# A hybrid encoder layer on one core: the scan's output step in its PSUM banks, six groups with both pairs of chunks in one run, and a split last product

## The chip, the core and the metric

The kernel runs on one core of a Trainium2 chip. The metric is device time in microseconds (us), lower is better: one layer of an encoder on 512 tokens of width 1024, batch 1, in float32. An execution is timed from outside; the profile shows one execution of its own, whose span runs from its first to its last recorded instruction.

TensorE multiplies matrices into PSUM, in banks of 128 x 512 float32, of which there are eight. VectorE (DVE) and ScalarE (ACT) read and write SBUF and PSUM; in this kernel GpSimd (POOL) works on SBUF alone. SyncE (SP) issues nearly all transfers. Each engine takes its instructions in order and waits at semaphores for the others.

## The reference

The layer mixes tokens by two branches, a bidirectional chunked state-space scan ("SSD") and windowed attention, merges them by gates, projects, normalises, adds the residual, and then runs a squared-ReLU MLP. The change touches the end of the scan and the end of the MLP:

```python
def ssd_scan(x, dt, a, b, c):           # one direction, 4 chunks of 128 tokens, 8 groups g of 4 heads
    ...
    cb = jnp.einsum('bclgn,bcsgn->bcgls', c, b)
    y_diag = jnp.einsum('bcgls,bcgrls,bcsgrp->bclgrp', cb, decay, xdt)      # within a chunk
    ...
    y_off = jnp.einsum('bclgn,bcgrpn,bcgrl->bclgrp', c, prev, jnp.exp(a_cs))
    return (y_diag + y_off).reshape(Bsz, S, G, R, P)

def ssd_branch(z, xbc, dt_raw, ...):
    ...
    y = y_fwd + y_bwd + xs * d_skip
    y = gated_rmsnorm(y, z, norm_w)     # u = y * silu(z); u * rsqrt(mean(u*u) per group) * w
    return y @ w_out

f = jnp.square(jax.nn.relu(h @ w_mlp_in)) @ w_mlp_out
x = x + rmsnorm(f, post_mlp_norm)
```

`prev` holds the states that enter each chunk from the ones before it. All matrix products are computed from float32 operands: each operand is split into a high part and a low part, and three products hi·hi, hi·lo, lo·hi are added in PSUM (`mm3`). The names `wh`/`wl`, `fh`/`fl`, `th`/`tl` are such pairs; `fc` holds both parts of one.

## The kernel before, in words

**What runs.** A list of "quanta" is built, each with weight chunks and a piece of TensorE work. The input projection comes first; then, for g = 0 to 7, six projections of the scan group g + 1 stand beside the scan steps of group g, attention heads, gates and the attention's output; then the scan's output projection, the output projection "o", the MLP's up projection, and its down projection in four parts, each a Winograd-Strassen product of seven half-size products. Part 3 is the program's end.

**Scan group g.** `prep(c)` makes for each of four chunks the decay matrix `m`. `load(c)` brings `E`, the factors exp(a_cs) of one or two directions (two for the two middle entries, so six 128x256 blocks per group). `off(j)` multiplies, for the pair j of two chunks, the entering states `pv` by `C` into two PSUM banks `yo`; `scaled(j)` (line 1207) has VectorE write `yo * E` over `E` in SBUF, which frees the bank. `diag(j)` multiplies `m` and `x` into one bank `yd` with 64-column tiles. `joined(j)` (line 1213) has VectorE add `yd` to `w` (which holds x times d_skip), then POOL add each block of `E` (line 1219) and multiply by the gate `z` (line 1220). ScalarE squares, POOL adds the squares (1227), and `rms` and `finish` normalise. `outs(0)` and `outs(1)` (line 1235) place these steps for the two pairs; in the groups of the table `JOINED` the first visit does only `off(0)` and `scaled(0)`, and the second all the rest of both pairs. `outs` also runs the attention's value products that are due (`ps<-pT,V` in a trace).

**Banks.** Three banks are called `pp` (projections), five `ps` (everything else). A name in a trace is the name of the tensor.

**The end.** In part 3 the seven products run in the order A11, A12, S2, S1, S4, S3, A22, each for two blocks of 128 tokens (u = 0, 1), 12 matmuls of 512 columns a block. They accumulate in banks X, Y and Z. After each block `gather` (line 1666) adds the bank to an SBUF tile `acc`. When the last product of an output block is in, `down_done` (line 1675) squares `acc` with a row sum on ScalarE (1686), adds the sums (1689, 1691), multiplies by the norm's gains into `ag` (1695), and, when both halves of a token row are there, has POOL raise the mean to -1/2 (1698) and VectorE compute `x1 + ag * r` (1701), which SP writes out (1702).

**Order.** After the program is written, `Planner` puts each engine's instructions in a fixed order by dependencies, estimated durations and due times; what an engine runs next is then fixed, and it waits if the operand is late. Uses of one PSUM bank count as dependent on each other whatever their columns.

## Time and profile before

| | us |
|---|---|
| median of 3 runs (1071.22 to 1071.63) | 1071.27 |
| the profiled execution, timed from outside | 1071.39 |
| its span | 1069.4 |
| HBM read | 128.68 MB |

A row of the profile reads "line engine operation out<-in, shapes, xcount", then busy time and the mean of one. A row of the timeline reads: start, duration, engine, line, operation, and in brackets the idle time before it with the engine that ended it. "PEld" is TensorE's loading of the stationary operand, beside its matmuls. Matmuls are pipelined: the duration that stands in a row (about 0.39 us for 512 columns) overlaps the next one, so the distance of two starts tells what one costs. Some matmul records are missing from a trace.

### The profile page before, as it was taken

To read this page: it belongs to the slowest core of one execution; us is meant where nothing else is said; L and a number is where in the kernel's file an instruction comes from. 1 tells how busy PE (TensorE), PEld (TensorE's weight loads), DVE (VectorE), ACT (ScalarE), POOL (GpSimd) and SP (SyncE) were. 2 spreads that over 40 slices of the span, in tenths; PEclk is the share of its full clock that TensorE was granted. 3 is DMA by queue.
4 is the path that set the end of the run, shared out by engine and by line. 5 is a ranking of instruction groups with operands and counts; after the bars stand their busy time and mean duration, and the time that the engine had idled before them with its cause. 6 is when DMAs were issued, how large, how long until landed. Compare 5 with 4: busy or idle time off the path is not lost.

```text
span 1069.4 us, 16514 instructions
## 1 busy us (share of the span) xinstructions
PE 1059.7 (99%) x5542; PEld 894.1 (84%) x5542; DVE 774.7 (72%) x1352; ACT 658.4 (62%) x1411; POOL 770.3 (72%) x862
## 2 busy tenths in 40 slices
PE   9999999999999999999999999999999999999997
PEld 8888888888888888888888888889888888888885
DVE  5987877886895878788876536798764584584698
ACT  7875776686686767677787414566645444444552
POOL 4746457477577698998789956214688897898994
PEclk9999999999999999999999999999999999999999
DMA  8433323433433526253535444317222421424122
GB/s 323 136 128 110 98 99 115 132 99 118 127 110 124 158 94 173 75 178 126 176 88 176 156 142 138 128 65 242 90 69 80 157 79 65 155 97 150 67 99 78
DMA packets 62084, 134.24 MB, mean 126 GB/s; under 512 B 9128, under 2 KB 18984, under 8 KB 62000
## 3 DMA queue, kind: packets, MB, share of 16 engines
q1 hardware_dynamic: 61712, 132.96, 38.3%
q8 instruction: 43, 0.70, 0.3%
q14 instruction: 41, 0.34, 0.1%
q10 hardware_dynamic: 288, 0.23, 0.1%
HBM read 128.68 MB, written 4.49 MB: 125 GB/s over the span
## 4 chain that ended last, share of the span: by engine, by line
PE 90%; DVE 5%; DMA 2%; ACT 2%; issue 1%; POOL 0%; DVEq 0%; POOLq 0%; ACTq 0%
PE pp L455 57%; PE ps L455 30%; PE ps L459 3%; DMA row<-in_row 1%; DMA x<-in_x 1%; DVE P L952 1%; DVE u L1014 1%; DMA xt<-in_xt 0%; DVE h L746 0%; POOL wl L1621 0%; DMA wr<-in_wv 0%; ACT P L946 0%; DVE dtw L817 0%; DVE Q L911 0%; DVE x L1416 0%
## 5 line engine op out<-in xcount | busy, mean ns | idle before, releaser
L534 POOL TENSOR_TENSOR wl<-wr,wh 128x342 fp32r<-128x342 f32 (+2 forms) x390 | 385.7, 1004 | 209.5 <-ACT wh L530 200.8
L455 PE MATMUL pp<-h,wh 128*128 128x512 f32 (+1 forms) x1664 | 505.5, 385 | 0.0
L455 PEld LDWEIGHTS pp<-h,wh 128*128 128x128 f32 x1664 | 306.4, 188 | 59.4 <-issue 0.7
L455 PE MATMUL pp<-h,wl 128*128 128x512 f32 (+1 forms) x832 | 320.8, 386 | 0.0
L530 ACT CAST wh<-wr 128x1024 fp32r<-128x1024 f32 (+1 forms) x130 | 135.0, 1040 | 127.6 <-PE pp L455 102.6
L455 PEld LDWEIGHTS pp<-h,wl 128*128 128x128 f32 x832 | 156.4, 188 | 30.5 <-issue 0.2
L1621 POOL TENSOR_TENSOR wl<-wd,wh 128x256 fp32r<-128x256 f32 x158 | 133.4, 882 | 12.5 <-ACT wh L1618 12.1
L1618 ACT CAST wh<-wd 128x512 fp32r<-128x512 f32 x92 | 53.3, 618 | 36.2 <-PE ps L455 19.3
L455 PE MATMUL ps<-wl,fh 128*128 128x512 f32 x184 | 71.7, 390 | 0.1
L455 PE MATMUL ps<-wh,fh 128*128 128x512 f32 x184 | 71.6, 389 | 0.0
L455 PE MATMUL ps<-wh,fl 128*128 128x512 f32 x184 | 71.6, 389 | 0.0
L1456 DVE SCALAR_TENSOR_TENSOR pp<-pp,r 128x256 f32<-128x256 f32 (+1 forms) x31 | 17.3, 559 | 64.6 <-ACT r L1453 64.5
L1180 ACT ACTIVATE n<-cb,tables 128x128 f32<-128x128 f32 x128 | 49.1, 392 | 17.6 <-DVE cb L1171 17.6
L1014 DVE SCALAR_TENSOR_TENSOR u<-pp,cv,u 128x510 f32<-128x510 f32 (+1 forms) x64 | 47.8, 746 | 7.1 <-ACT u L1010 5.7
L1181 ACT ACTIVATE m<-cb,tables 128x128 f32<-128x128 f32 x128 | 48.8, 389 | 2.3 <-DVE cb L1171 2.3
L1219 POOL TENSOR_TENSOR w<-w,E 128x256 f32<-128x256 f32 x48 | 41.7, 880 | 7.5 <-DVE w L1215 6.5
L1174 POOL TENSOR_TENSOR rb<-rb,tables 128x512 f32<-128x512 f32 x32 | 37.8, 1185 | 7.3 <-DMA rb<-csT 6.0
L1176 ACT ACTIVATE rf<-rf,tables 128x128 f32<-128x128 f32 x128 | 41.9, 392 | 1.8 <-DMA rf<-csT 1.7
L1112 POOL TENSOR_TENSOR xd<-x,tables 128x256 f32<-128x256 f32 x48 | 34.8, 742 | 9.1 <-ACT x L1037 3.5
L455 PEld LDWEIGHTS ps<-wl,fh 128*128 128x128 f32 x184 | 34.5, 188 | 8.0 <-POOL wl L1621 0.6
L455 PEld LDWEIGHTS ps<-wh,fh 128*128 128x128 f32 x184 | 34.5, 188 | 7.2
L455 PEld LDWEIGHTS ps<-wh,fl 128*128 128x128 f32 x184 | 34.5, 188 | 7.0
(291 smaller groups left out, 2262.4 us busy)
## 6 DMA issues: line engine op xcount, KB each, us to landing
wr<-in_w_in_b SPq DMA_DIRECT2D x74, 512.0 KB, 4.7
wr<-in_w_mlp_in_b SPq DMA_DIRECT2D x32, 512.0 KB, 3.3
wd<-in_w_mlp_out SPq DMA_DIRECT2D x64, 256.0 KB, 3.6
rb<-csT SPq DMA_DIRECT2D x32, 256.0 KB, 4.1
rf<-csT SPq DMA_DIRECT2D x32, 256.0 KB, 4.3
wr<-in_w_ssd_out_b SPq DMA_DIRECT2D x13, 512.0 KB
x<-in_x SPq DMA_DIRECT2D x16, 256.0 KB, 4.3
E<-csE SPq DMA_DIRECT2D x32, 128.0 KB, 4.4
```

The costliest lines, as they stand in the source:

```text
L455: self.nc.tensor.matmul(out, lhsT, rhs, start=start, stop=stop, skip_group_check=more)
L530: self.nc.scalar.copy(hi[:, :m], raw)
L534: self.nc.gpsimd.tensor_tensor(lo[:, c], raw[:, c], hi[:, c].bitcast(F32), op=ALU.subtract)
L1014: nc.vector.scalar_tensor_tensor(u[:, a:e], ps[:, a + d:e + d], self.wtap(t, b), u[:, a:e], op0=ALU.mult, op1=ALU.add)
L1112: nc.gpsimd.tensor_tensor(v4(xd[:, d * 256:(d + 1) * 256]), v4(xs(c)), by_dir(self.coef, c)[:, d].unsqueeze(2).to_broadcast([128, 4, 64]), ...
L1174: nc.gpsimd.tensor_tensor(v4(rb), v4(rb), cs[:, 1].unsqueeze(2).to_broadcast([128, 4, 128]), op=ALU.subtract)
L1176: nc.scalar.activation(v4(rf)[:, h], v4(rf)[:, h], AF.Identity, bias=ncs[:, 0, h:h + 1])
L1180: nc.scalar.activation(v4(n)[:, h], cb[:, 0], AF.Copy, scale=dt[:, 0, h:h + 1])
L1181: nc.scalar.activation(v4(m)[:, h], cb[:, 1], AF.Copy, scale=dt[:, 1, h:h + 1])
L1219: nc.gpsimd.tensor_tensor(wc, wc, E[:, d], op=ALU.add)
L1618: nc.scalar.copy(hi, src)
L1621: (nc.vector if q == 512 else nc.gpsimd).tensor_tensor(lo[:, c], src[:, c], hi[:, c].bitcast(F32), op=ALU.subtract)
```

## The change

Three things. (1) For all eight groups, `scaled` multiplies inside the bank `yo`, gives `E` back at once, and VectorE adds each block of `yo` to `w`; `joined` adds `w` into the bank `yd` and VectorE writes `yd * z` to `w`. POOL's two lines are left without callers. `scaled(j)` now stands right behind `off(j)`. (2) Groups 0 and 5 join 3, 4, 6, 7 in `JOINED`. (3) The last three products of part 3 become one quantum with their six blocks in the order of `CLOSING`. The last block is done in two halves of 256 columns, the far half in a bank of its own. Where a bank is not used again, `acc` is added into the bank, not the bank to `acc` (`summed`), and the norm's gains are multiplied in place there; otherwise they go to a `pp` bank. The unchanged context that the diff leaves out is marked by "...".

```diff
...
 PAIRS = (1, 0), (2, 3)
-JOINED = (3, 4, 6, 7)
+JOINED = (0, 3, 4, 5, 6, 7)
 ALONE = (7,)
...
 BACK = 3
+IN_BANK = range(8)
+END, END_BANK = 256, "ps"
+CLOSING = ("S4", 0), ("S3", 0), ("S4", 1), ("A22", 0), ("S3", 1), ("A22", 1)
 PIECES = 3
...
                 dd = slice(dirs[3 - c][0], dirs[3 - c][-1] + 1)
-                E = ch[c]["E"]
-                nc.vector.tensor_tensor(E[:, dd], ch[c]["yo"][:, dd], E[:, dd], op=ALU.mult)
+                E, yo = ch[c]["E"], ch[c]["yo"]
+                if g not in IN_BANK:
+                    nc.vector.tensor_tensor(E[:, dd], yo[:, dd], E[:, dd], op=ALU.mult)
+                    continue
+                nc.vector.tensor_tensor(yo[:, dd], yo[:, dd], E[:, dd], op=ALU.mult)
+                put(E)
+                for d in dirs[3 - c]:
+                    wc = st["w"][j][:, c % 2]
+                    nc.vector.tensor_tensor(wc, yo[:, d], wc, op=ALU.add)
 
         def joined(j):
             w = st["w"][j]
-            nc.vector.tensor_tensor(w, ch[j]["yd"], w, op=ALU.add)
-            for c in PAIRS[j]:
-                wc, E = w[:, c % 2], ch[c]["E"]
-                for d in dirs[3 - c]:
-                    nc.gpsimd.tensor_tensor(wc, wc, E[:, d], op=ALU.add)
-                nc.gpsimd.tensor_tensor(wc, wc, st["z"][j][:, c % 2], op=ALU.mult)
-                put(E)
+            if g in IN_BANK:
+                yd = ch[j]["yd"]
+                nc.vector.tensor_tensor(yd, yd, w, op=ALU.add)
+                nc.vector.tensor_tensor(w, yd, st["z"][j], op=ALU.mult)
+            else:
+                nc.vector.tensor_tensor(w, ch[j]["yd"], w, op=ALU.add)
+                for c in PAIRS[j]:
+                    wc, E = w[:, c % 2], ch[c]["E"]
+                    for d in dirs[3 - c]:
+                        nc.gpsimd.tensor_tensor(wc, wc, E[:, d], op=ALU.add)
+                    nc.gpsimd.tensor_tensor(wc, wc, st["z"][j][:, c % 2], op=ALU.mult)
+                    put(E)
             if "ssq" not in st:
...
                 off(j)
+                if g in IN_BANK or j == 0 and g in JOINED:
+                    scaled(j)
                 if j == 0 and g in JOINED:
-                    scaled(0)
                     return
...
                     diag(i)
-                scaled(j)
+                if g not in IN_BANK:
+                    scaled(j)
                 for i in js:
...
 
-        def product(a, b, bank, first, to):
+        def multiply(a, ps, parts, u, col, first):
+            tok = slice(u * 128, (u + 1) * 128)
+            for k in range(4):
+                hi, lo = self.f[part, k][a]
+                w = [x[:, col] for x in parts[k // 2][0][k % 2]]
+                self.mm3(ps, (hi[:, tok], lo[:, tok]), w, first and k == 0, k == 3, not first)
+
+        def ends(a, t, j):
+            return part == 3 and a == [p for p in order if (t, j) in products[p][3]][-1]
+
+        def summed(a, t, j, u, ps, col):
+            if not self.complete:
+                self.g4 = self.norm_rows("post_mlp_norm")
+            stays = a == [p for p in order if products[p][1] == products[a][1]][-1]
+            if stays:
+                total = out = ps
+                self.nc.vector.tensor_tensor(ps[:, col], self.acc[2 * t + u, j][:, col], ps[:, col], op=ALU.add)
+            else:
+                self.gather(2 * t + u, j, ps, col)
+                total, out = self.acc[2 * t + u, j], self.bank("pp")
+            self.down_done(2 * t + u, j, col, total, out)
+
+        def step(a, parts, u):
+            _, bank, first, to = products[a]
+            if first and not u:
+                banks[bank] = [self.bank("pp" if (part, bank) in PP_BANKS else "ps") for _ in range(2)]
+            col, ps = slice(0, 512), banks[bank][u]
+            multiply(a, ps, parts, u, col, first)
+            for t, j in to:
+                if part == "o":
+                    self.mixed(2 * t + u, j, ps, col)
+                    continue
+                if ends(a, t, j):
+                    summed(a, t, j, u, ps, col)
+                else:
+                    self.gather(2 * t + u, j, ps, col)
+
+        def last_step(a, parts, u):
+            _, bank, _, ((t, j),) = products[a]
+            near, far, ps, more = slice(0, END), slice(END, 512), banks[bank][u], self.bank(END_BANK)
+            multiply(a, more[:, far], parts, u, far, True)
+            self.gather(2 * t + u, j, ps, far)
+            summed(a, t, j, u, more, far)
+            multiply(a, ps[:, near], parts, u, near, False)
+            summed(a, t, j, u, ps, near)
+
+        def free(a, parts):
+            for f in self.held[part]:
+                put(*f.pop(a, ()))
+            for tiles, far in parts:
+                if far:
+                    put(*tiles[0], *tiles[1])
+
+        def product(a, b, *_):
             def run(parts):
-                if first:
-                    banks[bank] = [self.bank("pp" if (part, bank) in PP_BANKS else "ps") for _ in range(2)]
-                col = slice(0, 512)
                 for u in range(2):
-                    tok, ps = slice(u * 128, (u + 1) * 128), banks[bank][u]
-                    for k in range(4):
-                        hi, lo = self.f[part, k][a]
-                        self.mm3(ps, (hi[:, tok], lo[:, tok]), parts[k // 2][0][k % 2], first and k == 0, k == 3, not first)
-                    for t, j in to:
-                        if part == "o":
-                            self.mixed(2 * t + u, j, ps, col)
-                            continue
-                        self.gather(2 * t + u, j, ps, col)
-                        if part == 3 and a == [p for p in order if (t, j) in products[p][3]][-1]:
-                            if not self.complete:
-                                self.g4 = self.norm_rows("post_mlp_norm")
-                            self.down_done(2 * t + u, j, col)
-                for f in self.held[part]:
-                    put(*f.pop(a, ()))
-                for tiles, far in parts:
-                    if far:
-                        put(*tiles[0], *tiles[1])
+                    step(a, parts, u)
+                free(a, parts)
             return Quantum([chunk(b, c) for c in range(2)], run)
+
+        def closing():
+            names = [a for a in order if a in {a for a, _ in CLOSING}]
+
+            def run(parts):
+                parts = {a: parts[2 * i:2 * i + 2] for i, a in enumerate(names)}
+                for n, (a, u) in enumerate(CLOSING):
+                    (last_step if n == len(CLOSING) - 1 else step)(a, parts[a], u)
+                for a in names:
+                    free(a, parts[a])
+            return Quantum([chunk(products[a][0], c) for a in names for c in range(2)], run)
 
...
                     self.at(len(self.quanta) - lead - (k < 2), lambda name=name, k=k: load(name, k))
-        return [product(a, *products[a]) for a in order]
+        together = {a for a, _ in CLOSING} if part == 3 else ()
+        return [product(a, *products[a]) for a in order if a not in together] + ([closing()] if together else [])
 
...
 
-    def down_done(self, t, j, col):
+    def down_done(self, t, j, col, total, out):
 
...
         n = len(seen)
-        seen.append((j, col))
+        seen.append((j, col, out))
         ssq, rs = self.fs[0][:, t], self.fs[1][:, 2 * t:2 * t + 2]
-        a = self.acc[t, j][:, col]
         junk = self.slots.get("junk")
-        nc.scalar.activation(junk[:, col], a, AF.Square, accum_out=ssq[:, n:n + 1])
+        nc.scalar.activation(junk[:, col], total[:, col], AF.Square, accum_out=ssq[:, n:n + 1])
         self.slots.put(junk)
...
                                            op0=ALU.mult, op1=ALU.add)
-        if col.start == 0:
-            self.ag[t, j] = self.slots.get("ag")
-        nc.vector.tensor_tensor(self.ag[t, j][:, col], a, self.g4[j][:, col], op=ALU.mult)
-        if sum(c.stop - c.start for _, c in seen) == D:
+        nc.vector.tensor_tensor(out[:, col], total[:, col], self.g4[j][:, col], op=ALU.mult)
+        if sum(c.stop - c.start for _, c, _ in seen) == D:
             r = rs[:, n % 2:n % 2 + 1]
             nc.gpsimd.tensor_tensor(r, r, self.mhalf, op=ALU.pow)
-            for i, c in seen:
+            for i, c, out in seen:
                 x1 = self.x1[t][i]
-                nc.vector.scalar_tensor_tensor(x1[:, c], self.ag[t, i][:, c], r, x1[:, c], op0=ALU.mult, op1=ALU.add)
+                nc.vector.scalar_tensor_tensor(x1[:, c], out[:, c], r, x1[:, c], op0=ALU.mult, op1=ALU.add)
                 nc.sync.dma_start(self.out[0, t * 128:(t + 1) * 128, i * 512 + c.start:i * 512 + c.stop], x1[:, c])
-
```

The places that matter to the order of work follow; names are tensors with their numbers, and line numbers behind + are the changed file's.

VectorE in scan group 5, second pair (`E_5488`, `E_5602` its factors, `C_5768`/`C_5756` the convolution of the next projection, which reads a `pp` bank). Before:

```order
L1014 SCALAR_TENSOR_TENSOR C_5768<-pp_5711,cv,C_5768 128x510
L1014 SCALAR_TENSOR_TENSOR C_5768<-pp_5711,cv,C_5768 128x511
L1211 TENSOR_TENSOR E_5488<-ps_5724,E_5488 128x512
L1215 TENSOR_TENSOR w_5093<-ps_5732,w_5093 128x512
L1014 SCALAR_TENSOR_TENSOR C_5768<-pp_5711,cv,C_5768 128x511
L1014 SCALAR_TENSOR_TENSOR C_5768<-pp_5711,cv,C_5768 128x510
L1211 TENSOR_TENSOR E_5602<-ps_5729,E_5602 128x256
```

There one use of the bank `ps_5724` or `ps_5729` by VectorE frees it, and POOL works on from SBUF. Changed:

```order
L1217 TENSOR_TENSOR ps_5698<-ps_5698,E_5478 128x512
L1185 TENSOR_TENSOR m_5617<-m_5617,n_5618 128x512
L1017 SCALAR_TENSOR_TENSOR B_5648<-pp_5600,cv,B_5648 128x510
L1221 TENSOR_TENSOR w_5088<-ps_5698,w_5088 128x256 x2
L1024 SCALAR_TENSOR_TENSOR B_5648<-th_5654,B_5648 128x512
L1180 TENSOR_TENSOR rf_5572<-rf_5572,rb_5573 128x512
L1217 TENSOR_TENSOR ps_5703<-ps_5703,E_5576 128x256
L1221 TENSOR_TENSOR w_5088<-ps_5703,w_5088 128x256
```

A bank `yo` is now used by VectorE two or three times, with other work between, before it is free again.

VectorE, from the last full block's first sum to the last instruction. Before (`ps_11045`, `ps_11046` are the banks of the last two blocks):

```order
L1691 SCALAR_TENSOR_TENSOR frs_11114<-fsq_11113,frs_11114 128x1
L1673 TENSOR_TENSOR acc_9196<-acc_9196,ps_11046 128x512
L1701 SCALAR_TENSOR_TENSOR x_1233_11220<-ag_11316,frs_11114,x_1233_11220 128x512
L1695 TENSOR_TENSOR ag_11375<-acc_9196,post_mlp_norm_11109 128x512
L1701 SCALAR_TENSOR_TENSOR x_1232_11218<-ag_11352,frs_11114,x_1232_11218 128x512
L1701 SCALAR_TENSOR_TENSOR x_1235_11224<-ag_11334,frs_11114,x_1235_11224 128x512
L1701 SCALAR_TENSOR_TENSOR x_1234_11222<-ag_11375,frs_11114,x_1234_11222 128x512
```

There the last sum and the last two results are 512 columns wide. Changed (`ps_11338` is the far half's own bank, `ps_11030` that of the near half):

```order
L1736 TENSOR_TENSOR acc_9180<-acc_9180,ps_11030 128x256
L1660 TENSOR_TENSOR ps_11338<-acc_9180,ps_11338 128x256
L1761 SCALAR_TENSOR_TENSOR x_1231_11202<-pp_11271,frs_11098,x_1231_11202 128x512
L1660 TENSOR_TENSOR ps_11030<-acc_9180,ps_11030 128x256
L1753 SCALAR_TENSOR_TENSOR frs_11098<-fsq_11097,frs_11098 128x1
L1761 SCALAR_TENSOR_TENSOR x_1230_11200<-ps_11029,frs_11098,x_1230_11200 128x512
L1755 TENSOR_TENSOR ps_11338<-ps_11338,post_mlp_norm_11092 128x256
L1755 TENSOR_TENSOR ps_11030<-ps_11030,post_mlp_norm_11092 128x256
L1761 SCALAR_TENSOR_TENSOR x_1233_11206<-pp_11333,frs_11098,x_1233_11206 128x512
L1761 SCALAR_TENSOR_TENSOR x_1232_11204<-ps_11338,frs_11098,x_1232_11204 128x256
L1761 SCALAR_TENSOR_TENSOR x_1232_11204<-ps_11030,frs_11098,x_1232_11204 128x256
```

Behind the last matmul VectorE now handles 256 columns where it handled 512, but writes three results for the last 128 tokens, not two.

## Prediction

> **What bounds the kernel now.** I read the page first (busy shares, slices, chain), then what TensorE waited for, then stages of the span, then the end instruction by instruction.
>
> ```profile
> PE 1059.7 (99%) x5542; PEld 894.1 (84%) x5542; DVE 774.7 (72%) x1352; ACT 658.4 (62%) x1411; POOL 770.3 (72%) x862
> PEclk9999999999999999999999999999999999999999
> PE 90%; DVE 5%; DMA 2%; ACT 2%; issue 1%; POOL 0%; DVEq 0%; POOLq 0%; ACTq 0%
> PE pp L455 <- DVE two L674: 1.0, 1, 1.0
> PE ps L459 <- DVE P L952: 0.5, 1, 0.5
> PEld ps L455 <- issue: 2.9, 11, 0.4
> ```
>
> TensorE is busy all through at the full clock, and its waits for other engines come to 1.5 us. A busy share alone proves little here, because the durations of matmuls overlap; what proves it is the distance of their starts. In the chain of waits, 96 matmuls of 512 columns took 21.79 us, 0.227 each, and 72 of 256 columns 8.87 us, 0.123 each:
>
> ```profile
> 744.78 8.87 PE pp L455 x72
> 756.52 21.79 PE pp L455 x96
> ```
>
> That pace holds nearly everywhere. So what leaves POOL or shortens a chain in the middle gains nothing by itself. Three things can move the time: TensorE's own work, a new wait of TensorE, and what follows its last matmul. The stages show how loaded the helpers are:
>
> ```profile
> 350.00:563.00 213.00, 213.00 (x1128) 178.55 (x1127) 173.75 (x244) 156.17 (x353) 182.19 (x199) 1.00 0.45 133
> 1045.24:1061.56 16.32, 16.32 (x73) 13.32 (x71) 15.29 (x28) 4.86 (x12) 8.50 (x10) 1.00 0.17 64
> 1061.56:1069.40 7.84, 0.16 (x1) 0.00 (x0) 4.10 (x7) 0.72 (x2) 1.17 (x2) 0.68 0.36 134
> ```
>
> The columns are length, then PE, PEld, DVE, ACT and POOL busy. In the densest part of the scan VectorE is busy 173.75 of 213 us (82%); in the last six blocks (1045.24 to 1061.56) 15.29 of 16.32, which is nearly full; and 7.84 us run after the last matmul has been issued.
>
> **Part 1: the scan's output step.** POOL loses both its lines and VectorE gains them, in PSUM:
>
> ```profile
> L1219 POOL TENSOR_TENSOR w<-w,E 128x256 f32<-128x256 f32 x48 | 41.7, 880 | 7.5 <-DVE w L1215 6.5
> L1220 POOL TENSOR_TENSOR w<-w,z 128x256 f32<-128x256 f32 x32 | 25.2, 810 | 0.0
> L1211 DVE TENSOR_TENSOR E<-ps,E 128x256 f32<-128x256 f32 x16 | 6.6, 413 | 0.0
> L1215 DVE TENSOR_TENSOR w<-ps,w 128x512 f32<-128x512 f32 x16 | 10.9, 681 | 0.5 <-PE ps L455 0.5
> L1456 DVE SCALAR_TENSOR_TENSOR pp<-pp,r 128x512 f32<-128x512 f32 x15 | 10.5, 697 | 43.4 <-ACT r L1453 43.3
> ```
>
> POOL is relieved of 41.7 + 25.2 = 66.9 us. VectorE gets 48 additions of 256 columns at 0.413 (19.8 us) and 16 gate products of 512 columns at 0.681 (10.9 us), 30.7 us in all, 3.84 per group. The product that now stays in the bank costs what it did: writing in place in PSUM took 0.697 for 512 columns (line 1456) against 0.681. Four groups of output steps lie in the stretch 350 to 563, so VectorE goes there from 173.75 to about 189 of 213 us, 89%. It is not full, and TensorE's next projections cover the work; I take 0 for it. POOL's relief is hidden too, since TensorE did not wait for it. The cost if the cover is gone is the slower rival below; a gain here is excluded, there being no wait in the scan to take away beyond fractions of a us.
>
> **Part 2: groups 0 and 5 in one run.** TensorE saves a visit to the 64-column products. What a visit costs beyond its matmuls is read at one of group 5:
>
> ```profile
> 489.12 0.39 PE L455 MATMUL pp<-h,wh 128*128 128x512 f32 x1
> 489.44 1.09 PE L455 MATMUL ps<-m,x 128*64 128x128 f32 x16
> 490.46 0.66 PE L459 MATMUL ps<-ident,B 128*128 128x128 f32 x4
> ...
> 128.26 1.50 PE L455 MATMUL ps<-C,pv 128*128 128x128 f32 x12
> 129.69 4.59 PE L455 MATMUL ps<-pT,V 128*64 128x128 f32 x80
> 134.10 1.04 PE L455 MATMUL ps<-m,x 128*64 128x128 f32 x16
> 135.08 0.49 PE L455 MATMUL ps<-C,B 128*128 128x128 f32 x2
> ```
>
> The matmul at 489.12 is over at 489.35 by the pace, and the products start at 489.44: 0.09. They take 1.02 to the next start, where the same 16 inside a longer stretch (134.10 to 135.08) take 0.98: 0.04. Two visits fewer are about -0.3 us. Bounds: 0, if a projection slips between, and -0.5, if the changes back to the split products go too. The price is that four `m` are held longer and the value products of group 0 come later, with its second pair; TensorE has other work there, so 0.
>
> **Part 3: the end.** The last block in halves is 24 matmuls at 0.123 in place of 12 at 0.227: +0.2 us (2.95 - 2.72), so the last issue ends at 1061.79, not 1061.56. Its weights are wanted no earlier than they were; those of S3 and of A22 one block (2.72 us) earlier. POOL makes their last pieces:
>
> ```profile
> 1050.02 1.89 POOL L1621 TENSOR_TENSOR wl<-wd,wh 128x256 fp32r<-128x256 f32 x2
> 1061.20 0.54 POOL L1698 TENSOR_TENSOR frs<-frs,mhalf 128x1 f32<-128x1 f32 x1 [7.46 <-DVE frs L1691]
> 1063.86 0.98 POOL L1698 TENSOR_TENSOR frs<-frs,mhalf 128x1 f32<-128x1 f32 x1 [2.11 <-DVE frs L1691]
> ```
>
> They are ready at 1051.91; A22's first block now starts three blocks after 1045.24, at 1053.4, so 0. Now the chain behind the last matmul:
>
> ```profile
> 1061.75 0.69 DVE L1673 TENSOR_TENSOR acc<-acc,ps 128x512 f32<-128x512 f32 x1 [0.63 <-PE ps L455]
> 1062.36 0.74 DVE L1701 SCALAR_TENSOR_TENSOR x<-ag,frs,x 128x512 f32<-128x512 f32 x1
> 1062.47 0.63 ACT L1686 ACTIVATE junk<-acc 128x512 f32<-128x512 f32 x1 [1.99 <-DVE acc L1673]
> 1063.01 0.18 ACT L1686 ACTIVATION_READ_ACCUMULATOR junk<-acc 128x1 f32 x1
> 1063.62 0.15 DVE L1691 SCALAR_TENSOR_TENSOR frs<-fsq,frs 128x1 f32<-128x1 f32 x1
> 1063.69 0.74 DVE L1701 SCALAR_TENSOR_TENSOR x<-ag,frs,x 128x512 f32<-128x512 f32 x1
> 1064.88 1.42 DVE L1701 SCALAR_TENSOR_TENSOR x<-ag,frs,x 128x512 f32<-128x512 f32 x2 [0.44 <-POOL frs L1698]
> ```
>
> Counted from the issue end: the sum starts after 0.19, the square 0.72 after that, the mean's sum at 2.06, POOL's power at 2.30 for 0.98, the results from 3.32 to 4.74, and the span ends 3.10 later. Changed: the half sum (0.41, the 256-column row) ends at 0.60, the half square starts at 0.63. Its time I estimate between the 512-column row (0.63) and half of it, 0.42, and the read of the row sum ends 0.09 after that (1063.01 + 0.18 against 1062.47 + 0.63): 1.14. VectorE is meanwhile in a result of 512 columns that stands ahead (0.67 to the next start, as two take 1.42 and one 0.75), and takes the mean's sum at about 1.27. The power starts 0.24 later, at 1.51. For its length the trace has two values: 0.54 where VectorE stood still, 0.98 where VectorE read two SBUF operands beside it (`ag` and `x` at 1063.69). In the changed order an operand of VectorE's work beside it is a bank; I take 0.54 and keep 0.98 as a bound. That gives 2.05. The three results (0.67, then two of 256 columns: 0.41 by the row of that width, the first less the same overlap of 0.06) run from 2.09 to 3.52, and the tail of 3.10 is kept. So 6.62 in place of 7.84: -1.2 us. With 0.98 it is -0.8, and if the squares are not shortened -1.0.
>
> The Trainium skill, "SBUF — State Buffer", section "SBUF: two separate sides", has a rule for the two lengths: a VectorE operation with two SBUF inputs and a GpSimd operation that reads SBUF lock each other out of one port pair. By that rule 0.54 is the one to take, and the rows agree. Against the change speaks "Perfetto Trace Analysis", section "Optimizing Scalar/DVE Operations": VectorE's overhead is about 125 ns on PSUM, 60 ns on SBUF. By it the six VectorE operations of the new tail that use banks would lose up to 6 x 65 ns, 0.4 us; the row at line 1215 (0.681 from a bank) beside the sum in the tail (0.69) leaves no room to tell, and my sum goes by the rows.
>
> **The sum.** 1069.4 - 0.3 + 0.2 - 1.2 = 1068.1 us of span. Around it lie 1071.39 - 1069.4 = 1.99 us: 1070.1, and as the median shown is 0.12 below the profiled execution, **1070.0 us**, 0.12% less.
>
> **The rivals.**
>
> *The end gains nothing (about 1071.0).* The near half's matmuls write the bank from which VectorE must first fetch the far half's old sum; dependencies go by whole banks. They are due 2.95 + 0.19 us at most after the previous block, while VectorE has a full sum, that fetch and 15.29 us of other work in 16.32. By the starts of the rows (0.61 per 512-column sum) the fetch is over about 0.2 us ahead of time. If VectorE is 1 us late, TensorE waits that long, and the gain of the end is spent: 1070.0 + 1.0. For it: VectorE is the fullest engine there. Against it: its chores at 1042 to 1049 are unchanged.
>
> *Slower: VectorE is late with banks in the scan (about 1075).* Only five `ps` banks exist. A pair of `off` gave its second bank back after 0.68 + 0.41 = 1.09 us of VectorE; it now takes three additions more (1.24 us) behind it, and other VectorE work stands between in the new order. The two `yd` banks are used twice, 0.68 longer each. If TensorE has to sit out one such delay of 1.24 in each of the four dense groups, that is +5.0 us: 1075.0. It decides from the point where less matmul work than VectorE's queue stands between `off` and the next use of a `ps` bank. For it: 89% of VectorE, strict order on each engine, and joined runs that want four banks at once. Against it: TensorE waited 0.5 us for VectorE in the whole scan, and projections of 5.44 us (24 x 0.227) in `pp` banks stand between.
>
> *Faster by more (about 1069.0).* The issue gaps of 2.9 us before weight loads, and with them the waits at the changes of kind, fall by a third with fewer visits, another -1.0. For it speaks only that joined groups already run without them.
>
> That the change doesn't do what it says in the scan, so that POOL keeps the work, is ruled out by its order, which has no such line left.
>
> **How the numbers follow.** Forecast 0.45, the end gains nothing 0.18, slower 0.27, faster by more 0.10. The forecast's own range, from the tail's bounds and the visits' bounds, is 1069.4 to 1070.9. For 8 in 10 I go from 1069.0 to 1074.0: below it lies half of the faster case, above it about half of the slower one. A measurement of this kernel tells about 0.2% (2.1 us) from no change, so 1069.1 and 1073.4 are the limits: faster 0.10, same 0.62, slower 0.28.
>
> **What would show it.** Right: TensorE's waits in the scan stay under 2 us with VectorE near 90% in the dense stretch and POOL down by some 67 us; the last power takes 0.54; from the last matmul's issue to the span's end it is about 6.6 us. Wrong in the end: a wait of the 256-column matmuls for VectorE's fetch, or a power of 0.98. Wrong in the scan: a row of TensorE, or of its weight loads, waiting for VectorE at lines of `scaled` or `joined`, repeated by group. The forecast falls altogether if matmuls of 512 columns no longer start 0.227 us apart.

## The result, and the profile after

| | before | after |
|---|---|---|
| median, us | 1071.24 (16 runs, 1070.72 to 1071.63) | **1069.24** (16 runs, 1068.66 to 1070.15) |
| span of the profiled execution, us | 1069.4 | 1067.3 |

The ratio is 0.9981, 95% interval 0.9974 to 0.9988: the change saves 2.0 us, 0.19%. The forecast was 1070.0, a gain of 1.2. The sign was right and the size was not: 1069.24 lies near the lower end of the range that was given 8 in 10 (1069.0 to 1074.0), and just below the forecast's own (1069.4 to 1070.9).

The page of the changed kernel, busy shares and chain:

```profile
PE 1058.8 (99%) x5554; PEld 894.9 (84%) x5554; DVE 784.5 (74%) x1421; ACT 658.5 (62%) x1413; POOL 699.9 (66%) x782
PE 92%; DVE 3%; ACT 2%; DMA 2%; issue 1%; SPq 0%; DVEq 0%; POOL 0%; ACTq 0%
```

TensorE issues 12 matmuls more (the last block in 24, not 12) and bounds the kernel as before. POOL lost 70.4 us of busy time (770.3 to 699.9). VectorE gained only 9.8.

What TensorE waited for in the changed kernel (total, times, longest):

```profile
PE pp L458 <- DVE two L677: 1.0, 1, 1.0
PE ps L462 <- DVE P L955: 0.5, 1, 0.5
```

These are the two rows of before. No row of the scan's output step and none of the last block has appeared among TensorE's matmuls. The dense part of the scan and the last six blocks of the changed kernel (columns as before: length, PE, PEld, DVE, ACT, POOL):

```profile
349.20:562.20 213.00, 213.00 (x1130) 178.90 (x1129) 183.76 (x282) 156.57 (x354) 156.43 (x166) 1.00 0.46 137
1044.08:1060.40 16.32, 16.32 (x85) 13.94 (x83) 15.80 (x31) 4.61 (x13) 7.51 (x10) 1.00 0.17 64
1060.40:1067.30 6.90, 0.16 (x2) 0.00 (x0) 3.41 (x9) 0.47 (x2) 0.54 (x1) 0.73 0.42 152
```

VectorE is at 183.76 of 213 us (86%) in the dense part, and TensorE still fills it. The end after the last issue takes 6.90 in place of 7.84.

To see where the 2.1 us of span went, both executions are cut at the same matmuls of the program. Before:

```profile
123.19 0.28 PE L455 MATMUL ps<-KH,Q 128*128 128x256 f32 x1
178.02 0.39 PE L455 MATMUL ps<-sh,ones_r 128*128 128x512 f32 x1
258.67 0.39 PE L455 MATMUL ps<-sh,ones_r 128*128 128x512 f32 x1
612.94 0.39 PE L455 MATMUL ps<-sh,ones_r 128*128 128x512 f32 x1
756.00 0.40 PE L455 MATMUL ps<-h,th 128*128 128x256 f32 x2
```

The changed kernel:

```profile
123.32 0.28 PE L458 MATMUL ps<-KH,Q 128*128 128x256 f32 x1
177.86 0.39 PE L458 MATMUL ps<-sh,ones_r 128*128 128x512 f32 x1
258.16 0.39 PE L458 MATMUL ps<-sh,ones_r 128*128 128x512 f32 x1
611.97 0.39 PE L458 MATMUL ps<-sh,ones_r 128*128 128x512 f32 x1
755.11 0.40 PE L458 MATMUL ps<-h,th 128*128 128x256 f32 x2
1060.28 0.28 PE L458 MATMUL ps<-wh,fc 128*128 128x256 f32 x1
```

The first row is the start of an attention head's scores inside group 0's scan. `ps<-sh,ones_r` is the norm product that closes a scan group: the rows show those of group 0, group 1 and group 7. The `ps<-h,th` row is a landmark in the MLP's up projection; the last is the last matmul, issued for 0.123 us (before: 1061.33 and 0.227). Differences of these starts give the stretches:

| stretch | before | after | difference |
|---|---|---|---|
| start to the scores' row | 123.19 | 123.32 | +0.13 |
| group 0's scan | 54.83 | 54.54 | -0.29 |
| group 1's scan | 80.65 | 80.30 | -0.35 |
| groups 2 to 7 (group 5 among them) | 354.27 | 353.81 | -0.46 |
| to the landmark in the MLP | 143.06 | 143.14 | +0.08 |
| to the end of the last issue | 305.56 | 305.29 | -0.27 |
| from there to the span's end | 7.84 | 6.90 | -0.94 |

The scan thus gave 1.10, the last part 1.21. The experiments tell which edit each row belongs to.

### The profile page after: what moved, and what is told of

The parts are those of the page before. It is cut to its first block, busy times and chain, and to the rows that moved or that the text cites. A ratio compares the mean times of both kernels' runs of the same rounds, so it can differ in the third digit from the quotient of the medians.

```text
span 1067.3 us, 16535 instructions
## 1 busy us (share of the span) xinstructions
PE 1058.8 (99%) x5554; PEld 894.9 (84%) x5554; DVE 784.5 (74%) x1421; ACT 658.5 (62%) x1413; POOL 699.9 (66%) x782
## 4 chain that ended last, share of the span: by engine, by line
PE 92%; DVE 3%; ACT 2%; DMA 2%; issue 1%; SPq 0%; DVEq 0%; POOL 0%; ACTq 0%
PE pp L458 58%; PE ps L458 31%; PE ps L462 3%; DMA wr<-in_w_in_b 1%; DVE u L1017 1%; DMA wr<-in_wv 1%; DVE h L749 0%; ACT wh L533 0%; ACT P L949 0%; DVE dtw L820 0%; DVE x L1433 0%; DVE Q L914 0%; DVE Q L909 0%; DVE P L955 0%; DVE acc L1412 0%
## 5 line engine op out<-in xcount | busy, mean ns | idle before, releaser
L949 ACT ACTIVATE P<-P,mx 128x256 f32<-128x256 f32 (+1 forms) x64 | 35.4, 556 | 4.1 <-DVE mx L941 3.8
```

The lines of the kernel that those rows point to most:

```text
L949: nc.scalar.activation(p[:, :w], p[:, :w], AF.Exp, bias=mx[:, n:n + 1], scale=-1.0, accum_out=sm[:, n:n + 1])
```

## The experiments

Every kernel was profiled and timed beside runs of the kernel before. The last column is the ratio to it with its 95% interval, the others are the stretches above, in us.

| kernel | start | group 0 | group 1 | 2 to 7 | to last issue | end | median | ratio |
|---|---|---|---|---|---|---|---|---|
| before | 123.19 | 54.83 | 80.65 | 354.27 | 305.56 | 7.84 | | |
| after | 123.32 | 54.54 | 80.30 | 353.81 | 305.29 | 6.90 | 1069.24 | 0.9981 (0.9974 to 0.9988) |
| only the end | 123.09 | 54.83 | 80.62 | 354.26 | 305.81 | 6.84 | 1070.59 | 0.9995 (0.9986 to 1.0003) |
| only the banks | 123.11 | 54.83 | 80.66 | 354.25 | 305.11 | 7.85 | 1070.89 | 0.9996 (0.9987 to 1.0005) |
| banks and groups 0, 5 | 124.29 | 54.54 | 80.29 | 353.87 | 305.16 | 7.90 | 1070.67 | 0.9993 (0.9985 to 1.0002) |
| only group 5 joined | 124.43 | 54.83 | 80.64 | 355.44 | 305.13 | 7.82 | 1072.37 | 1.0011 (1.0002 to 1.0020) |
| after, without group 0 | 123.28 | 54.82 | 80.67 | 353.87 | 305.26 | 6.92 | 1069.88 | 0.9986 (0.9977 to 0.9995) |
| after, without group 5 | 122.83 | 54.54 | 80.48 | 354.19 | 305.30 | 6.85 | 1069.52 | 0.9983 (0.9974 to 0.9992) |
| after, last block whole | 124.65 | 54.54 | 81.37 | 353.83 | 306.21 | 6.99 | 1071.53 | 1.0000 (0.9991 to 1.0009) |
| after, gains to SBUF | 123.00 | 54.54 | 81.04 | 353.85 | 305.42 | 6.86 | 1069.65 | 0.9984 (0.9975 to 0.9993) |
| after, old order of blocks | 122.63 | 54.54 | 80.34 | 353.83 | 305.28 | 7.28 | 1069.23 | 0.9980 (0.9971 to 0.9989) |
| after, last sums in SBUF | 122.85 | 54.54 | 80.31 | 353.83 | 305.22 | 7.49 | 1069.62 | 0.9986 (0.9977 to 0.9995) |
| before, again | 123.25 | 54.83 | 80.61 | 354.27 | 305.55 | 7.83 | 1071.30 | 0.9998 (0.9988 to 1.0008) |
| after, again | 122.67 | 54.55 | 81.94 | 353.83 | 305.30 | 6.92 | 1069.65 | 0.9983 (0.9973 to 0.9993) |

The stretch to the landmark, 143.01 to 143.14 in all of them, is left out. Most stretches repeat within 0.1 us from kernel to kernel where the order there is the same, though medians of 11 runs are uncertain by about 1 us; so the stretches carry the reading. Two do not repeat. The start ranges from 122.63 to 124.65, although TensorE's order up to the scores' row is the same in all of them; the two kernels that were profiled twice differ by 0.06 and by 0.65 there. Whether the start belongs to the execution or to the built kernel is not shown. Group 1's scan scatters in the kernels with group 0 joined, and only there.

### Only the end; only the banks

The end alone: the changed kernel with both scan tables as before.

```diff
-JOINED = (0, 3, 4, 5, 6, 7)
+JOINED = (3, 4, 6, 7)
-IN_BANK = range(8)
+IN_BANK = ()
```

> The split and reordered end alone, with the scan as before. Theory A (the time came from two separate sources, the scan's order on TensorE and the chain behind the last matmul): last matmul issued about 0.2 us later than before's, 0.9 to 1.2 us less from there to the span's end, so 1070.2 to 1070.4 us. Theory B (the scan's relief of POOL also lets the end start earlier): the end alone gains under 0.5 us, 1070.8 or more.

The end fell from 7.84 to 6.84 and the scan's stretches stayed those of before. The halves cost 0.25 in the stretch before it, near the 0.2 of the forecast. By the stretches this is theory A; the median, 1070.59, lies between the two theories and decides nothing.

The banks alone: the kernel before with part (1) of the change and nothing else.

```diff
+IN_BANK = range(8)
...
-        nc.vector.tensor_tensor(E[:, dd], ch[c]["yo"][:, dd], E[:, dd], op=ALU.mult)
+        nc.vector.tensor_tensor(yo[:, dd], yo[:, dd], E[:, dd], op=ALU.mult)
+        put(E)
...
+                nc.vector.tensor_tensor(wc, yo[:, d], wc, op=ALU.add)
```

> The scan's output step in its PSUM banks by VectorE for all eight groups, JOINED and the end as before. Forecast's theory: no change, 1071.2 us, TensorE's issue pace and waits as before. Rival C (moving the step off POOL changes TensorE's order so that it changes kind less often, or takes small waits away): TensorE reaches the MLP 0.4 us or more earlier, 1070.8 us or less. Slower rival (VectorE late with banks): waits of TensorE at the step's lines, over 1072 us.

The three stretches of the scan are those of before within 0.03 us: in the scan, part (1) by itself neither gains nor costs, as the forecast had it. But the stretch to the last issue is 0.45 shorter, in a part of the program that this edit does not touch. The trace of before shows why, at 954 us:

```profile
954.86 0.19 PEld L455 LDWEIGHTS ps<-wl,fh 128*128 128x128 f32 x1 [0.57 <-POOL wl L1621]
954.86 0.50 PE L455 MATMUL ps<-wl,fh 128*128 128x512 f32 x1
```

A weight load waits for POOL's split of a weight piece, and the matmul before it is followed after 0.54 us (954.32 to 954.86), not 0.23. The wait is in the kernel before, in its repetition and in "only the end", and in no other kernel of the table. So it belongs to the kernel and not to the execution. It is gone with the banks alone and also with group 5's join alone; what either of them changes in POOL's work around 950 us was not followed further.

### Banks and joins; group 5 joined without the banks

The banks with the changed table of joins, the end as before:

```diff
-JOINED = (3, 4, 6, 7)
+JOINED = (0, 3, 4, 5, 6, 7)
+IN_BANK = range(8)
...
```

> The scan's part of the change whole (in the banks, groups 0 and 5 joined), the end as before. Forecast's theory: two visits to the 64-column products fewer, 0.3 us, 1070.9 us. Rival C: 0.9 us or more, 1070.3 us or less, as TensorE's start of the MLP in the changed kernel's trace lies 0.9 us earlier than before's.

Group 0's scan fell by 0.29, group 1's by 0.36, groups 2 to 7 by 0.40: more than the forecast's theory, and about what rival C expected. The median shows only 0.5 us. The profiled execution began late (124.29 at the scores' row); how the others began is not known.

The kernel before with group 5 joined and the step still in SBUF:

```diff
-JOINED = (3, 4, 6, 7)
+JOINED = (3, 4, 5, 6, 7)
```

> Group 5 joins the groups that do both pairs in one run, all else as before. Forecast's theory: one visit fewer, 0.13 us, 1071.1 us, no difference that can be told. Rival (a joined run saves the changes of kind around it too): 0.3 to 0.5 us, seen as an earlier start of everything behind group 5.

Groups 2 to 7 took 355.44, 1.17 more than before and 1.57 more than with the banks; both theories had expected a gain. Group 5's own scan, from group 4's norm product to its own, did gain: 53.33 against 53.61. The loss stands behind it, at group 6's norm product, in rows of POOL, ScalarE and TensorE:

```profile
558.94 3.73 POOL L1220 TENSOR_TENSOR w<-w,z 128x256 f32<-128x256 f32 x4
562.63 1.53 POOL L1227 TENSOR_TENSOR ssq<-sq 128x256 f32<-128x256 f32 x2
564.20 0.62 ACT L472 CAST sh<-ssq 128x512 fp32r<-128x512 f32 x1
564.87 0.50 PE L455 MATMUL ps<-sh,ones_r 128*128 128x512 f32 x1 [0.17 <-ACT sh L472]
566.82 0.50 PE L455 MATMUL ps<-xh,bt 128*128 128x512 f32 x1 [0.42 <-ACT xh L1116]
```

POOL's part of the output step (lines 1219 and 1220) runs from 553.92 to 562.67; the sum of squares, its cast `sh` and the norm product follow at once, and then `xh`, which ScalarE casts from the `xd` that POOL makes next. The two matmuls start 0.56 and 0.91 us after those ahead of them, where the pace is 0.227: 1.0 us lost. In the kernel before, `sh` was ready at 555.29 and wanted at 557.86. POOL's busy share alone would not show this: it is 53.86 of 55 us here (558 to 613), 38.13 in a like 55 us with the banks and the same join, but 52.38 in the kernel before, which loses nothing there. With the banks the two lines are gone, and no such wait of TensorE's matmuls appears. So the relief of POOL, which I had set to nothing, is what lets group 5 run joined without a loss. The same trial with group 0 was not made, so whether its join needs the banks too is not shown.

### Each join taken out of the changed kernel

```diff
-JOINED = (0, 3, 4, 5, 6, 7)
+JOINED = (3, 4, 5, 6, 7)
```

> The changed kernel without group 0 in JOINED. If each of the two groups saves its own visit, half of the scan's gain is lost: from group 0's norm product to the last group's, 0.8 us gained by the changed kernel's trace, about 0.4 us here, and 1069.6 us in all. If the gain is group 5's alone: 1069.2 us, as the changed kernel. If it is group 0's alone: 1070.0 us.

```diff
-JOINED = (0, 3, 4, 5, 6, 7)
+JOINED = (0, 3, 4, 6, 7)
```

> The changed kernel without group 5 in JOINED. Mirror of the run before it: about 1069.6 us if each group saves its own part, 1070.0 us if it was all group 5's, 1069.2 us if it was all group 0's.

Without group 0's join, group 0's scan goes back to 54.82 and group 1's to 80.67; without group 5's, groups 2 to 7 go back to 354.19 (group 5's own scan from 53.19 to 53.58). Each stretch follows its own table entry and no other, but for group 1's scatter. The medians, 0.6 and 0.3 above the changed kernel's, are too near to it to tell.

The rows say where most of the 0.29 and the 0.39 is. In the kernel without group 5's join, the first of its two runs of products, with the projections (`pp<-h`) on both sides:

```profile
461.69 0.39 PE L458 MATMUL pp<-h,wl 128*128 128x512 f32 x1
462.01 1.09 PE L458 MATMUL ps<-m,x 128*64 128x128 f32 x16
463.03 0.71 PE L458 MATMUL ps<-C,B 128*128 128x128 f32 x4
463.50 0.71 PE L458 MATMUL pp<-h,wh 128*128 128x512 f32 x2
```

and in the changed kernel, where this visit is gone, the one run that is left:

```profile
486.95 1.97 PE L458 MATMUL ps<-m,x 128*64 128x128 f32 x32
488.85 0.66 PE L462 MATMUL ps<-ident,B 128*128 128x128 f32 x4
```

The way in costs 0.09 (461.69 to 462.01 is 0.32, where the pace is 0.227). The way back costs as much: the two projections from 463.50 take until 464.05, 0.55 in place of 0.45. The 32 products in one run take 1.90 to the next start, two runs of 16 took 1.02 each: 0.14. Together that is 0.33 of the 0.39. Between group 4's norm product and group 5's, TensorE leaves the 512-column projections for 128-column work four times in the changed order (at 455.82, 476.25, 486.95 and 501.91) and five times without group 5's join. In the kernel before it did so six times (456.33, 461.81, 466.44, 478.24, 489.44 and 502.84) and took 53.61, no longer than the 53.58 with five; so the number of visits alone does not give the time.

In group 0 no visit is saved. Its first run of products (134.10) stands inside a longer visit, and behind the scores TensorE leaves the projections eight times with the join, seven times without. What falls is the products, 1.85 in one run (154.04 to 155.89) for 0.98 + 1.03 in two (134.10 and 154.85), 0.16, and changes of kind inside a visit: 12 products `C,pv` took 1.43 to the next start when the 64-column value products followed (128.26 to 129.69), and take 1.33 now that `C,B` follows (128.39 to 129.72).

### The last block whole; the gains in SBUF

```diff
-                    (last_step if n == len(CLOSING) - 1 else step)(a, parts[a], u)
+                    step(a, parts[a], u)
```

> The changed kernel with the last block in one piece of 512 columns, in the order of CLOSING and with the sums in the bank. TensorE saves 0.2 us, the chain behind it has full sums and squares: by the forecast's terms the sum (0.28) and the square (0.2) come back, two results take 1.4 in place of three in 1.45, so 0.2 to 0.4 us slower than the changed kernel, 1069.5 us. If the halves gain nothing: 1069.2 us or less.

This kernel was no faster than before, 2 us above what was expected. In its last six blocks VectorE's sum of the previous block, and TensorE's next block in the same bank:

```profile
1060.11 0.69 DVE L1736 TENSOR_TENSOR acc<-acc,ps 128x512 f32<-128x512 f32 x1
1060.85 0.50 PE L458 MATMUL ps<-th,fc 128*128 128x512 f32 x1 [0.78 <-DVE acc L1736]
```

TensorE waits 0.78 us until VectorE has fetched the bank: the mechanism of the rival "the end gains nothing", which the changed kernel escapes because its far half has a bank of its own and runs 1.48 us (12 x 0.123) while VectorE fetches. The end of this kernel, 6.99, is barely longer than 6.90. So in the new order of blocks the halves are worth the covered wait (net 306.21 - 305.29 = 0.92), and hardly the shorter chain. The wait comes with the new order, in which the last block directly follows the one before it in the same bank: the kernels with the end of before took 305.11 and 305.16 without it. These stretches explain 1.0 of the 2.3 us between the two medians. In the profiled execution the start and group 1's scan took 1.33 and 1.07 more, although every engine has the same order as in the changed kernel up to 1057 us. All 11 runs of this kernel (1070.72 and more) lie above the 16 of the changed one (1070.15 and less; its 8 later runs reach 1070.87), so the rest is hardly chance alone; its cause stays open.

To test the lock that I had assumed behind the two lengths of POOL's power, the gains' products were written to SBUF:

```diff
-                total, out = self.acc[2 * t + u, j], self.bank("pp")
-            self.down_done(2 * t + u, j, col, total, out)
+                total, out = self.acc[2 * t + u, j], None
+            if not self.sbuf.get((t, u, j)):
+                self.sbuf[t, u, j] = self.slots.get("ag")
+            self.down_done(2 * t + u, j, col, total, self.sbuf[t, u, j])
```

> The changed kernel, but the products with the norm's gains are written to SBUF tiles, so that VectorE's results beside POOL's last power read two SBUF operands again. If that pairing is what makes the power long (0.98 against 0.54 us), the last power takes 0.98 or starts late, and the span is 0.3 to 0.5 us longer, 1069.6 us. If the power's length comes from something else: 0.54 again and no change.

The power stayed at 0.54 and the end at 6.86. That decides nothing: the two VectorE operations beside the power still read the sum from a bank. A later trial closed that gap.

### The order of the last blocks; the last sums in SBUF; both kernels again

```diff
-CLOSING = ("S4", 0), ("S3", 0), ("S4", 1), ("A22", 0), ("S3", 1), ("A22", 1)
+CLOSING = ("S4", 0), ("S4", 1), ("S3", 0), ("S3", 1), ("A22", 0), ("A22", 1)
```

> The changed kernel with the last six blocks in the order of before (each product's two token tiles one after the other), halves kept. If the new order of those blocks is worth something, TensorE meets a wait for VectorE's sum again (a row of TensorE or of its weight loads waiting for acc of 0.2 us or more in 1040 to 1061) and the median is 1069.7 or more; if the order only matters for how many weight tiles are held, the median is 1069.2 to 1069.5 as the changed kernel's and no such row appears.

No wait came back, and the median is the changed kernel's. But the end took 7.28, not 6.90, and the timeline shows what stands in it. VectorE in this kernel, after the last half sum:

```profile
1060.26 0.74 DVE L1761 SCALAR_TENSOR_TENSOR x<-pp,frs,x 128x512 f32<-128x512 f32 x1
...
1060.99 0.74 DVE L1761 SCALAR_TENSOR_TENSOR x<-ps,frs,x 128x512 f32<-128x512 f32 x1
...
1062.39 0.75 DVE L1755 TENSOR_TENSOR ps<-ps,post_mlp_norm 128x256 f32<-128x256 f32 x2
```

The other rows of tokens are finished later in this order, so both of their results (1060.26 and 1060.99) stand behind the last half sum (at 1059.92), and the last gains come at 1062.39, behind the power; in the changed kernel only one result stands there, and the gains run beside the power. The profile puts 0.38 us on the new order. The median does not show it, and cannot tell so little.

```diff
-            stays = a == [p for p in order if products[p][1] == products[a][1]][-1]
+            stays = False
```

> The changed kernel with the last sums kept in the SBUF tiles acc and the gains' products in SBUF too, so that VectorE's two products of 256 columns beside POOL's last power read two SBUF operands each. If two SBUF operands on VectorE lengthen POOL's power (0.98 in the kernel before, 0.54 in the changed one), the last power takes 0.9 to 1.0, and the time from the last matmul's issue to the end is 7.2 to 7.4 in place of 6.90. If the 0.98 had another cause, the power stays at 0.54 and that stretch at 6.85 to 7.0.

This edit was made on top of the gains in SBUF. VectorE now reads two SBUF operands beside the last power:

```profile
1061.15 0.74 DVE L1763 SCALAR_TENSOR_TENSOR x<-ag,frs,x 128x512 f32<-128x512 f32 x1
1061.31 0.98 POOL L1760 TENSOR_TENSOR frs<-frs,mhalf 128x1 f32<-128x1 f32 x1 [3.87 <-DVE frs L1755]
1061.81 0.41 DVE L1757 TENSOR_TENSOR ag<-acc,post_mlp_norm 128x256 f32<-128x256 f32 x1
```

The power takes 0.98 again, and the end 7.49. With one operand in a bank it took 0.54 to 0.55 in every other kernel with the new end. By the rule of the Trainium skill, "SBUF — State Buffer", section "SBUF: two separate sides", a VectorE operation with two SBUF inputs and a GpSimd operation that reads SBUF lock each other out; the trace agrees, 0.98 against 0.54.

Last, both kernels once more, unchanged.

> The kernel before, unchanged. If TensorE's wait of 0.4 us at 954 us for POOL's split of a weight piece belongs to the kernel before, it is there again, and the stretch from the last group's norm product to the last matmul's issue end is 305.5 to 305.6; if it depends on the execution, the stretch may be 305.1 to 305.2 as in the second and third kernel run here. From the first group's norm product to the second's 80.6 to 80.7, from the second's to the last's 354.2 to 354.3 either way.

> The changed kernel, unchanged. If the joins are worth what the first execution shows, the second group's norm product follows the first's by 80.3 and the last's the second's by 353.8 to 353.9; if group 0's gain depends on the execution, the first of the two is up to 81.4 as in two kernels run here with group 0 joined. The wait at 954 us is absent, the stretch to the last issue's end 305.2 to 305.4, and the end after it 6.85 to 7.0.

The kernel before repeated in every stretch within 0.06 us, the wait at 954 us included. The changed kernel repeated in all but its start and one more: group 1's scan took 81.94, not 80.30, and more than the 81.4 that was allowed for. There its trace has a wait of TensorE for ScalarE:

```profile
209.12 0.33 SPq L1159 DMA_DIRECT2D rf<-csT  x1
215.10 1.28 ACT L1179 ACTIVATE rf<-rf,tables 128x128 f32<-128x128 f32 x4 [2.04 <-DMA rf<-csT]
219.22 0.48 ACT L966 COPY pT<-ps 128x384 f32<-128x384 f32 x1
219.75 0.39 PE L458 MATMUL ps<-KH,Q 128*128 128x256 f32 x1 [1.22 <-ACT pT L966]
```

ScalarE stands idle for 2.04 us until the load of `rf` (a row of the scan's decay table) is in, and behind it in ScalarE's order stands the copy `pT` that must empty a bank before the next scores. The same place in the changed kernel's first execution, where the load came in time:

```profile
209.77 0.33 SPq L1159 DMA_DIRECT2D rf<-csT  x1
213.88 1.28 ACT L1179 ACTIVATE rf<-rf,tables 128x128 f32<-128x128 f32 x4 [0.17 <-DMA rf<-csT]
218.06 0.48 ACT L966 COPY pT<-ps 128x384 f32<-128x384 f32 x1
```

and in the kernel before:

```profile
211.45 0.32 SPq L1156 DMA_DIRECT2D rf<-csT  x1
216.86 0.98 ACT L1176 ACTIVATE rf<-rf,tables 128x128 f32<-128x128 f32 x3
```

Before, the operands are wanted 5.4 us after the load's issue and nothing waits. With group 0 joined they are wanted some 4 us after it, and the load needed between about 4 and 6 us. All eight executions with group 0 joined line up by ScalarE's idle time before that row:

| kernel | idle for the load | group 1's scan |
|---|---|---|
| banks and groups 0, 5 | none shown | 80.29 |
| after; after with last sums in SBUF | 0.17; 0.17 | 80.30; 80.31 |
| after, old order of blocks | 0.30 | 80.34 |
| after, without group 5 | 0.37 | 80.48 |
| after, gains to SBUF | 1.02 | 81.04 |
| after, last block whole | 1.47 | 81.37 |
| after, again | 2.04 | 81.94 |

Beyond some 0.3 us of slack nearly all of the lateness goes into the time. In six executions without the join the stretch was 80.61 to 80.67. So group 0's join takes 0.35 off group 1's scan when the load is early and adds up to 1.3 when it is late. Where the 0.35 comes from was not followed row by row. Only the profiled executions show this; the spread of the timed runs does not settle how often it happens (1.5 us over 16 runs of the changed kernel, 0.9 over 16 and 2.2 over another 33 of the kernel before). An earlier issue of that load would be the next thing to try; it was not run. None of the kernels run beats the changed one by more than the medians can tell.

## Why the prediction was right in sign and short in size

**Part 1, the step in the banks: right at 0 in the scan.** "Only the banks" left each scan stretch within 0.03 us. The load on VectorE was overestimated: 189 of 213 us were forecast for the dense part, 183.76 came. The added work has the durations of the forecast, as the changed kernel's groups show (busy, mean ns):

```profile
L1221 DVE TENSOR_TENSOR w<-ps,w 128x256 f32<-128x256 f32 x48 | 19.4, 416 | 0.6
L1227 DVE TENSOR_TENSOR ps<-ps,w 128x512 f32<-128x512 f32 x16 | 11.0, 690 | 0.7 <-PE ps L458 0.7
```

What I left out is that much of VectorE's other work shrinks when POOL works less: summed over the groups that both kernels share in shape and count, by 16 us. One group of 32, before and then after, from the view by line:

```profile
L952 DVE TENSOR_SCALAR P<-P,sm 128x384 f32<-128x384 f32 x32 | 18.6, 615 | 0.0
```

```profile
L955 DVE TENSOR_SCALAR P<-P,sm 128x384 f32<-128x384 f32 x32 | 15.8, 526 | 0.0
```

What I had not seen either is that this part carries the next one: without POOL's relief, group 5's join costs 1.17. "What leaves POOL gains nothing" was thus wrong in two places outside the step itself, here and at the wait at 954 us below.

**Part 2, the joins: the step that failed.** The term was two visits fewer to the 64-column products, 0.09 + 0.04 each, -0.3. The runs show -0.29 for group 0 in its own scan and -0.39 for group 5, -0.7 in all. For group 5 the mechanism was right and the price too small: it had the way in, 0.09, but not the way back, which also costs 0.09, and it took 0.04 for two runs in place of one, which measured 0.14. The bound of -0.5 that I gave for "the changes back to the split products" did not cover it. For group 0 the mechanism was wrong: the very rows that I quoted show its first run inside a longer visit, and the join saves none there. That its 0.29 is of the forecast's size is luck. Setting the price of the later work at 0 missed a further thing: group 0's join re-times group 1's scan, for -0.35 or for a loss of up to 1.3 by the load of `rf`.

**Part 3, the end: right in mechanism, 0.3 short.** The chain went as worked out, until the results. The changed kernel's end:

```profile
1060.59 0.43 DVE L1660 TENSOR_TENSOR ps<-acc,ps 128x256 f32<-128x256 f32 x1 [0.20 <-PE ps L458]
...
1061.06 0.38 ACT L1748 ACTIVATE junk<-ps 128x256 f32<-128x256 f32 x1 [0.87 <-DVE ps L1660]
1061.66 0.15 DVE L1753 SCALAR_TENSOR_TENSOR frs<-fsq,frs 128x1 f32<-128x1 f32 x1
1061.73 0.76 DVE L1755 TENSOR_TENSOR ps<-ps,post_mlp_norm 128x256 f32<-128x256 f32 x2
1061.89 0.54 POOL L1758 TENSOR_TENSOR frs<-frs,mhalf 128x1 f32<-128x1 f32 x1 [4.20 <-DVE frs L1753]
1062.47 0.75 DVE L1761 SCALAR_TENSOR_TENSOR x<-pp,frs,x 128x512 f32<-128x512 f32 x1
1063.14 0.87 DVE L1761 SCALAR_TENSOR_TENSOR x<-ps,frs,x 128x256 f32<-128x256 f32 x2
```

Counted from the issue's end at 1060.40: the mean's sum at 1.26 (forecast 1.27), the power at 1.49 for 0.54 (1.51 and 0.54), the results from 2.07 (2.09). Then the results end at 3.61, not 3.52, and the span ends 3.29 later, not 3.10. I had kept the tail behind the last result unchanged; it was 0.19 longer. The width of the last results is not the reason: with the old order of blocks, and with the last sums in SBUF, the last two results are the same and the tail is 3.10 again. What lengthens it stays open. So -0.94 in place of -1.2. The extra matmuls cost 0.18 to 0.25 (0.2 forecast).

Against the end I had weighed a rule of the Trainium skill, "Perfetto Trace Analysis", section "Optimizing Scalar/DVE Operations", by which bank operands would lose up to 0.4 us. The runs do not bear it out: VectorE's 256-column gains took 424 ns from and to a bank in the changed kernel and 417 ns from and to SBUF with the last sums there.

**What was not in the sum.** The wait at 954 us, 0.45, went away with the scan's edits. I had argued that TensorE did not wait for POOL; but the list of its weight loads' waits had POOL's `wl` with 0.6 us, below the row that I quoted, and I did not ask what less work on POOL would do to it.

**The sum again.** Forecast: -0.3 + 0.2 - 1.2. Measured: -0.75 for the joins' own stretches, -0.35 for group 1, -0.27 to the last issue (+0.2 for the halves, -0.45 for the wait), -0.94 for the end; with the scatter of the start and of the stretch to the landmark (+0.13 and +0.08), -2.10 of span. The lower end of the forecast's own range, 1069.4, does not follow from the bounds given for it: the tail's and the visits' reach 1069.8 at the low end, and the measured time lies 0.6 below that.

**The rivals.** "The end gains nothing" has a real mechanism, shown with the whole last block, and the halves avoid it. "Slower, VectorE late in the scan" did not occur: no wait by group, and VectorE at 86%, not 89%. "Faster by more" gave the size nearly right for the wrong reason: the issue gaps before weight loads of `ps` matmuls were 2.9 and 2.1 in the first executions, but 2.3 in both repetitions; the joins and the wait at 954 us did it.

## What to carry to other kernels

Price a merged run by counting every change of kind in both orders, the way in and the way back, and look first whether the run stands in a visit of its own; here the joins gave over twice what was forecast. An edit that gains nothing alone can be what makes another affordable: test them together and each without the other. And when a step is moved forward, check how old the loads are that it reads: three of the eight profiled executions with group 0's join lost 0.7 us or more to a load that came late, and the first profile of the changed kernel did not show it.

## What the runs showed of the hardware

- The same load of 128x512 float32 at the same place in the program was there 4.1 us after its issue in one execution (213.88 - 209.77) and 5.98 us after it in another (215.10 - 209.12).
- VectorE's time for unchanged SBUF work can depend on POOL's: 615 to 526 ns for one shape when POOL lost 9% of its busy time, though a few groups rose (`xl<-xd,xh` of 512 columns from 1010 to 1075). The reverse shows in POOL's one-column power, 0.54 or 0.98.
- Between 512-column projections, a visit to 128-column work cost 0.09 us on the way back, and another 0.09 on the way in where 64-column tiles came first; 32 products with 64-column tiles took 1.85 to 1.90 us in one run and 2.01 to 2.04 in two.
- Most stretches of hundreds of us repeat within 0.1 us from execution to execution and across kernels with the same order there. Comparing such stretches told apart effects of 0.3 us that medians over 11 runs could not.
